# Layer 1 of a two-layer trunk: TensorE takes its work in the order of the program's text

## Chip, core and metric

The kernel runs on one core of a Trainium2 chip. The metric is the device time of one execution in microseconds. Engines are named as in the profile: PE (TensorE, matmuls), DVE (VectorE), ACT (ScalarE), POOL (GpSimd), SP (SyncE, which issues the DMAs).

## What is computed

Two layers over 1024 latent tokens and 256 context tokens, all 1024 wide, in fp32. Layer 0 is attention; layer 1 mixes a bidirectional gated DeltaNet (GDN, 4 heads of 128, chunks of 64 in the reference) with a bidirectional RG-LRU (width 512). Each ends in an output projection, a gate and a LayerNorm. The parts of layer 1 that matter here:

```python
qkv, z, b, a, xr, gr = _split(h @ w_in, REC_SPLITS)       # one input projection
qkv = silu(dwconv_centered(qkv, gdn_conv_w))              # centered, 4 taps
xl  = dwconv_centered(xr, lru_conv_w, lru_conv_b)
# GDN, for both directions:
decay = exp(where(causal, g_cum[..., :, None] - g_cum[..., None, :], -inf))
m   = where(strict, einsum('nbhid,nbhjd->nbhij', kb, k) * decay, 0.0)
sol = triangular_solve(m + eye, [v * beta, kb * exp(g_cum)])
# scan over chunks: v_new = u - w s;  o = q s + attn v_new;  s = s * gl + k_dec^T v_new
# RG-LRU, for both directions: h_t = a_t h_(t-1) + b_t, gates from xl @ w_gate
mix = concatenate([rms_norm(o) * silu(z), r * silu(gr)])
y   = mix @ w_out
```

## The kernel before

Each engine has its own stream of instructions. The program's text emits all of them in one sequence, and the framework's scheduler then makes an order for each engine: it goes by the place in the text but passes over an instruction whose inputs are not ready in the scheduler's own model of time, taking a later one first. `tc.manual_schedule(engines={...})`, entered as a context, switches this off for the engines named: their instructions keep the order of the text. Layer 0's attention already does so for PE and DVE, and closes that context before its output; layer 1 is left wholly to the scheduler.

The text of layer 1 has an order of its own. `seq` lists 24 pieces of the input projection (`xr`, `k`, `q`, `v`, `z`, `gr`, four each). `chunk` (line 1315) computes one piece for one stretch of tokens: 8 times `mm3`, which is three matmuls (high and low parts of the fp32 operands, `h1h`, `h1l`, `wf`), and after each `mm3` a call of `pump()`. That call lets background generators emit a little: first `lru_stream` for either direction (`lx` is the conv output read back from DRAM, `gw` the gate weights, `lw`/`lu` its tiles), then `gdn_prep` (line 1680), then `gdn`'s own levels. A planner with a rough clock for each engine (`Core.t`) decides when a generator may go on.

`gdn_prep` goes over 10 tiles of 128 tokens. For a tile and each direction, one matmul of the mask (`maskr`, `negi`) and one of the tile's decay rows (`dec`, read from the DRAM tensor `d_dec`) make the exponents, and ACT takes `D` = Exp of them. Gram matmuls of keys and queries (`kqt`) follow, and DVE multiplies both into `WX`. SP stores `WX` in `d_w` and, for latent tiles, `d_xa`. `dec` and `kqt` have two buffers each, so a tile's load waits until the tile before last has been read. After five tiles (0 to 4, 5 to 9) eight loads `ia` take the 32x32 diagonal blocks from `d_w`, and `inverse` (line 1780) inverts them, one direction on DVE and the other on POOL, step by step with `ia` and `itmp`; `it` is the transposed copy, stored as `d_bt`. The scan then loads `W`, `Tt`, `Tu`, `K`, `X`, `V`, combines blocks into 64x64 and larger inverses (`Tt,W`, `K,L`, `X,L`), and runs along the tokens with the state `S`. The output projection reads `wo`, `mh` and `ml`.

Other names: `xb` is a projection copied out of PSUM by ACT for the convolution, `yc` the convolution, `tm` a tile for results of z, gr and v (DVE evicts PSUM into it), `wf` the split weights (ACT rounds, DVE or POOL subtracts), `wfs` the weights as loaded. All compute instructions carry line 88, the helper that records them.

Of the kernel before, what the change touches and what calls it, by code (L numbers as in the profile page):

```python
# [111 lines left out]
class Trunk:  # L112
# [1164 lines left out]
    def layer1(self, es, eh):  # L1277
# [48 lines left out]
        def project(i, n0, evac):  # L1326
            for c in range(n0, 3):
                chunk(i, c, evac)
                if c == n0:
                    split(i + 2)  # L1330
                    load(i + 3)
                self.tick()
                self.pump()
# [11 lines left out]
        def copy_to(xb):  # L1345
            def evac(c, t0, n, acc):
                o = (1, 260, 772)[c]
                nc.scalar.copy(xb[:, o:o + n], acc[:, :n])

            return evac  # L1350

        def lru_input(f, xb):
            y = self.til(cp, [P, 1288], F32, "yc", bufs=3)
            self.conv(y, xb, 0, 1283, [rT[:, 48 + 4 * j + f:49 + 4 * j + f] for j in range(4)], rT[:, 64 + f:65 + f])
            nc.sync.dma_start(d["xl"][f, :, 0:256], y[:, 0:256])
            nc.sync.dma_start(d["xl"][f, :, 256:], y[:, 259:1283])
            self.xl_done.add(f)
# [26 lines left out]
        ef.close()  # L1384
        G = self.gdn(es)
        self.add(self.background(G))
        for i, (nm, f) in enumerate(seq):
            if i < 2:
                continue
            if nm in ("z", "gr"):  # L1390
                def evac(c, t0, n, acc):
                    if nm == "gr":
                        hs = self.til(cp, [P, 1288], F32, "yc", bufs=3)[:, 0:1024].rearrange("p (r t) -> p r t", r=2)
                        nc.sync.dma_start(hs, d["hs"][:, f, :, t0 - NCTX:t0 - NCTX + n].rearrange("r p t -> p r t"))
                        nc.vector.tensor_tensor(hs[:, 0], hs[:, 0], hs[:, 1], op=ALU.add)
                    zo = self.til(cp, [P, 512], F32, "tm", bufs=2)
                    nc.scalar.activation(zo[:, :n], acc[:, :n], AF.Tanh, scale=0.5)
                    nc.vector.scalar_tensor_tensor(zo[:, :n], zo[:, :n], 1.0, acc[:, :n], op0=ALU.add, op1=ALU.mult)
                    if nm == "gr":
                        nc.vector.tensor_tensor(zo, zo, hs[:, 0], op=ALU.mult)  # L1400
                    nc.sync.dma_start(d["z" if nm == "z" else "ylru"][f, :, t0 - NCTX:t0 - NCTX + n], zo)

                while nm == "gr" and not {(f, 0), (f, 1)} <= self.lru_done:
                    self.nc.t["p"] += 500.0
                    self.pump()
                project(i, 1, evac)
                continue
            n0 = 1 if nm == "q" else 0
            xb = xbs[:, i % 3]
            project(i, n0, copy_to(xb))  # L1410
            if nm == "xr":
                lru_input(f, xb)
            else:
                self.gdn_inputs(cp, nm, f, n0, xb)
            if f == 3 and nm == "k":
                self.defer(5, lambda: self.gdn_decay(cp))
            if f == 3 and nm == "q":
                self.q_done = True
                self.defer(5, lambda: self.gdn_scale(cp))
# [822 lines left out]
```

## Time and profile before

| | |
|---|---|
| time, median of 3 runs | 1845.74 us (1842.92 to 1847.27) |
| the profiled execution's own time | 1839.24 us |
| its span | 1837.5 us |
| mean granted clock of PE | 0.946 |
| busy: PE | 1657.8 us (90%) |
| busy: DVE | 1206.1 us (66%) |
| busy: ACT | 739.6 us (40%) |
| busy: POOL | 794.9 us (43%) |

The profile is one execution with every instruction's start and duration on its engine, and for idle time the event that ended it. The chain that ended last, followed back from the last instruction, lies 55% on PE and 20% on DVE. The change concerns what is emitted from about 1144 us on. In a timeline row, "[6.07 <-DMA dec<-d_dec]" means 6.07 us of idle time of that engine before the instruction, ended by that DMA; `x2` folds two instructions of one kind. In the page the granted clock is a share of full speed: 1.00 is 2.4 GHz, 0.50 is 1.2 GHz.

### The profile page before, as it was taken

What the parts mean: (1) busy time and instruction counts of PE and PEld (TensorE: products, weight loads), DVE (VectorE), ACT (ScalarE), POOL (GpSimd) and SP (SyncE); (2) the same over time, 40 slices, a digit from 0 to 9 for tenths busy, and PEclk for the clock granted to TensorE, in tenths of its full rate; (3) what the DMA queues carried; (4) which work ended last, traced back from release to release, by engine and by line L of the source; (5) the groups of instructions that cost most, each with busy time, mean ns of one, the idle gap of its engine ahead of it and who ended that gap; (6) DMA issues with size and microseconds to landing.
All of it is one profiled execution on the core that took longest, in us unless ns stands there. A gap on an engine that the chain in (4) does not pass through costs nothing.

```text
span 1837.5 us, 25439 instructions
## 1 busy us (share of the span) xinstructions
PE 1657.8 (90%) x9020; PEld 1210.1 (66%) x9020; DVE 1206.1 (66%) x2140; ACT 739.6 (40%) x1502; POOL 794.9 (43%) x727
## 2 busy tenths in 40 slices
PE   5999899997999998989989998988979858899997
PEld 2997776744555565655547886766856747789885
DVE  2657713236667767676774895888855498367887
ACT  2533401144555453434352443767643222234431
POOL 1432200075566666767542572233212673674121
PEclk8999999998999898989899998989988979999999
DMA  8343486163231101010044333333437447988552
GB/s 303 113 131 115 134 289 198 68 168 114 76 69 56 40 21 45 21 45 27 18 143 143 111 107 99 114 107 123 132 109 198 133 102 211 290 252 252 172 155 103
DMA packets 240995, 234.72 MB, mean 128 GB/s; under 512 B 62506, under 2 KB 188984, under 8 KB 238820
## 3 DMA queue, kind: packets, MB, share of 16 engines
q1 hardware_dynamic: 240868, 233.10, 41.6%
q8 instruction: 71, 1.16, 0.3%
q14 instruction: 56, 0.46, 0.1%
HBM read 163.37 MB, written 69.68 MB: 127 GB/s over the span
## 4 chain that ended last, share of the span: by engine, by line
PE 55%; DVE 20%; DMA 7%; issue 6%; ACT 4%; POOL 4%; SPq 2%; DVEq 0%; ACTq 0%; POOLq 0%
PE ps L88 39%; PE pb L88 10%; PE pv L88 7%; DVE yc L88 3%; DVE nb L88 2%; DVE f L88 2%; DMA modw<-in_mod_w 2%; DVE itmp L88 1%; DVE ia L88 1%; POOL ia L88 1%; DVE mx L88 1%; POOL itmp L88 1%; DVE lu L88 1%; DVE nsq L88 1%; DVE accv L88 1%
## 5 line engine op out<-in xcount | busy, mean ns | idle before, releaser
L88 DVE TENSOR_REDUCE mx<-ps 128x1 f32<-128x512 f32 (+1 forms) x384 | 207.3, 593 | 162.1 <-PE ps L88 160.1
L88 POOL TENSOR_TENSOR accp<-accp,pt 128x512 f32<-128x512 f32 x202 | 260.7, 1313 | 103.7 <-ACT pt L88 102.6
L88 ACT ACTIVATE pt<-pb 128x512 f32<-128x512 f32 (+1 forms) x352 | 194.5, 577 | 229.1 <-PE pb L88 225.0
L88 PE MATMUL ps<-h1h,wf 128*128 128x512 f32 (+1 forms) x864 | 277.9, 395 | 5.8 <-DVE tm L88 3.3
L88 PE MATMUL pb<-qh,kb 96*128 96x512 f32 (+4 forms) x528 | 213.2, 418 | 3.0 <-ACT pt L88 2.3
L88 PEld LDWEIGHTS ps<-h1h,wf 128*128 128x128 f32 x864 | 165.0, 197 | 41.7 <-issue 5.4
L88 PE MATMUL ps<-h1l,wf 128*128 128x512 f32 (+1 forms) x432 | 165.4, 383 | 0.0
L88 PEld LDWEIGHTS pb<-qh,kb 128*128 128x128 f32 (+2 forms) x528 | 102.3, 195 | 90.5 <-issue 65.5
L88 PE MATMUL ps<-kb,qh 128*128 128x512 f32 (+3 forms) x416 | 128.6, 386 | 32.0 <-DVE mx L88 28.7
L88 PE MATMUL pb<-ql,kb 66*128 66x512 f32 (+3 forms) x352 | 139.3, 397 | 0.0
L88 PEld LDWEIGHTS ps<-kb,qh 128*128 128x128 f32 (+1 forms) x416 | 80.9, 201 | 69.3 <-DVE mx L88 37.8
L88 POOL TENSOR_TENSOR accp<-pt,pt 128x512 f32<-128x512 f32 (+1 forms) x47 | 53.0, 1146 | 142.0 <-ACT pt L88 125.4
L88 DVE SCALAR_TENSOR_TENSOR yc<-xb,rT,yc 128x1283 f32<-128x1283 f32 (+1 forms) x48 | 88.1, 1845 | 26.8 <-ACT yc L88 26.4
L88 POOL TENSOR_TENSOR ml<-m,mh 128x512 fp32r<-128x512 f32 (+1 forms) x24 | 49.0, 2053 | 115.0 <-ACT mh L88 105.9
L88 PEld LDWEIGHTS ps<-h1l,wf 128*128 128x128 f32 x432 | 85.5, 198 | 16.7 <-issue 3.9
L88 PE MATMUL ps<-wl,hh 128*128 128x416 f32 (+2 forms) x240 | 84.6, 353 | 8.0 <-POOL wl L88 4.1
L88 PE MATMUL ps<-wh,hh 128*128 128x416 f32 (+2 forms) x240 | 85.4, 356 | 3.1 <-ACT wh L88 2.0
L88 PE MATMUL pv<-pt,vm 128*64 128x512 f32 (+1 forms) x352 | 85.1, 601 | 2.6 <-DVE mo L88 1.7
L88 PE MATMUL pv<-pt,vgqa 128*64 128x512 f32 (+1 forms) x352 | 85.3, 607 | 0.0
L88 PE MATMUL ps<-wh,hl 128*128 128x416 f32 (+2 forms) x240 | 84.0, 350 | 0.1
L88 PE MATMUL ps<-wo,mh 128*128 128x512 f32 x256 | 81.9, 398 | 2.0 <-ACT wo L88 1.6
L88 PE MATMUL ps<-w,mh 128*128 128x512 f32 x256 | 81.3, 398 | 1.1 <-DVE r L88 1.1
(373 smaller groups left out, 3723.9 us busy)
## 6 DMA issues: line engine op xcount, KB each, us to landing
modw<-in_mod_w SPq DMA_DIRECT2D x16, 1024.0 KB
wfs<-in_rec_w_in SPq DMA_DIRECT2D x22, 512.0 KB
modw<-in_mod_w SPq DMA_DIRECT2D x16, 512.0 KB
wst<-in_att_w_in SPq DMA_DIRECT2D x24, 256.0 KB
d_q<-qo SPq DMA_DIRECT2D x20, 256.0 KB
lx<-d_xl SPq DMA_DIRECT2D x8, 640.0 KB
d_w<-WX SPq DMA_DIRECT2D x20, 256.0 KB
W<-d_w SPq DMA_DIRECT2D x20, 256.0 KB
```

Of the source, the lines that this page charges most:

```text
L88: return fn(*args, **kw)
```

## The change

One line is added to `layer1`, after the first two pieces of the projection and after the background work has been registered:

```diff
@@ -1384,6 +1384,7 @@
         ef.close()
         G = self.gdn(es)
         self.add(self.background(G))
+        es.enter_context(self.tc.manual_schedule(engines={mybir.EngineType.PE}))
         for i, (nm, f) in enumerate(seq):
             if i < 2:
                 continue
```

`es` is the outermost context of the program, so this holds to its end: the rest of the input projection, the LRU, the GDN and the output. PE's instructions then stand as the text emits them. The other engines remain with the scheduler, whose model of time sees another PE, so that their orders change too, though not by rule. Numbers in the names below are those of the program's buffers; from about 9980 on those of the new program are higher by two. Line numbers after 1387 are higher by one.

PE, first tiles of `gdn_prep`. In the kernel before, a mask matmul of each direction, then projections and Gram products:

```order
L88 MATMUL ps_11492<-h1h_8679,wf_11157 128x512
L88 MATMUL ps_11496<-maskr_9582,negi_9580 128x512
L88 MATMUL ps_11501<-maskr_9582,negi_9580 128x512
L88 MATMUL ps_11492<-h1h_8679,wf_11157 128x512
L88 MATMUL ps_11492<-h1l_8680,wf_11157 128x512
L88 MATMUL ps_11492<-h1h_8679,wf_11157 128x512
L88 MATMUL ps_11511<-kqt_11482 128x128 x2
```

Further down in the same stream, where the decay matmuls of tiles 0 (`dec_11484`) and 1 (`dec_11489`) stand, and the transposes of a convolution (`ident`, `yc`) among them:

```order
L88 MATMUL ps_11492<-h1h_8679,wf_11157 128x512
L88 MATMUL ps_11567<-kqt_11487 128x128 x2
L88 MATMUL ps_11496<-dec_11484 128x512
L88 MATMUL ps_11501<-dec_11484 128x512
L88 MATMUL ps_11580<-ident_66,yc_11282 128x128 x2
L88 MATMUL ps_11542<-dec_11489 128x512
L88 MATMUL ps_11580<-ident_66,yc_11282 128x128 x2
```

In the changed kernel, the same place:

```order
L88 MATMUL ps_11494<-h1h_8679,wf_11159 128x512
L88 MATMUL ps_11498<-maskr_9582,negi_9580 128x512
L88 MATMUL ps_11498<-dec_11486 128x512
L88 MATMUL ps_11503<-maskr_9582,negi_9580 128x512
L88 MATMUL ps_11503<-dec_11486 128x512
L88 MATMUL ps_11494<-h1h_8679,wf_11159 128x512
L88 MATMUL ps_11494<-h1l_8680,wf_11159 128x512
L88 MATMUL ps_11494<-h1h_8679,wf_11159 128x512
L88 MATMUL ps_11513<-kqt_11484 128x128 x2
L88 MATMUL ps_11494<-h1h_8679,wf_11159 128x512
L88 MATMUL ps_11494<-h1l_8680,wf_11159 128x512
```

Tile 0's two `dec` matmuls moved up directly behind their `maskr`, ahead of 33 other matmuls or folds of matmuls.

SP, the stores of tile 3 (`WX_11698`, `WX_11699`) and the first of tile 4 (`WX_11747`); `dec_11848` is the decay load of tile 7 and `dec_11908` that of tile 8. Before:

```order
L1759 DMA d_w_8691<-WX_11698 128x4x128
L1761 DMA d_xa_8692<-WX_11698 512x1x128
L1759 DMA d_w_8691<-WX_11699 128x4x128
L1761 DMA d_xa_8692<-WX_11699 512x1x128
L1722 DMA kqt_11846<-d_kT_8689 128x4x128
L1725 DMA dec_11848<-d_dec_95 16x640 x2
L1727 DMA kqt_11846<-d_qT_8690 128x4x128
L1725 DMA dec_11908<-d_dec_95 16x640
L1759 DMA d_w_8691<-WX_11747 128x4x128
L1761 DMA d_xa_8692<-WX_11747 512x1x128
```

In the changed kernel, where tile 3 is `WX_11700` and `WX_11701` and tile 7 is `dec_11850`:

```order
L1726 DMA dec_11787<-d_dec_95 16x640
L1723 DMA kqt_11785<-d_kT_8689 128x4x128
L1726 DMA dec_11787<-d_dec_95 16x640
L1728 DMA kqt_11785<-d_qT_8690 128x4x128
L1726 DMA dec_11850<-d_dec_95 16x640
L1760 DMA d_w_8691<-WX_11700 128x4x128
L1762 DMA d_xa_8692<-WX_11700 512x1x128
L1760 DMA d_w_8691<-WX_11701 128x4x128
L1762 DMA d_xa_8692<-WX_11701 512x1x128
```

Half of tile 7's decay load moved ahead of tile 3's stores.

DVE, the end of its inverse: `ia_12201` is the second inverse's matrix, `tm_13036` an eviction of the gr projection and `wf_13157` a split of weights. Before:

```order
L88 SCALAR_TENSOR_TENSOR tm_13036<-tm_13036,ps_13008 128x512
L88 TENSOR_TENSOR ia_12201<-ia_12201,itmp_2957_12883 80x27x4
L88 TENSOR_TENSOR tm_13036<-tm_13036,yc_13033 128x512
L88 TENSOR_TENSOR itmp_2962_12908<-ia_12201 80x84
L88 MEMSET ia_12201 80x32
L88 TENSOR_TENSOR ia_12201<-ia_12201,itmp_2962_12908 80x28x3
L88 TENSOR_TENSOR itmp_2963_12917<-ia_12201 80x58
L88 TENSOR_TENSOR ia_12201<-ia_12201,itmp_2963_12917 80x29x2
L88 TENSOR_TENSOR itmp_2964_12926<-ia_12201 80x30
L88 TENSOR_TENSOR wf_13157<-wfs_13044,wf_13157 128x1024
L88 TENSOR_TENSOR ia_12201<-ia_12201,itmp_2964_12926 80x30
L88 COPY it_12937<-ia_12201 80x1024
```

In the changed kernel (`ia_12203`, `tm_13038`, `wf_13159`):

```order
L88 TENSOR_TENSOR itmp_2962_12910<-ia_12203 80x84
L88 MEMSET ia_12203 80x32
L88 TENSOR_TENSOR ia_12203<-ia_12203,itmp_2962_12910 80x28x3
L88 TENSOR_TENSOR itmp_2963_12919<-ia_12203 80x58
L88 TENSOR_TENSOR ia_12203<-ia_12203,itmp_2963_12919 80x29x2
L88 TENSOR_TENSOR itmp_2964_12928<-ia_12203 80x30
L88 TENSOR_TENSOR ia_12203<-ia_12203,itmp_2964_12928 80x30
L88 COPY it_12939<-ia_12203 80x1024
L88 SCALAR_TENSOR_TENSOR tm_13006<-tm_13006,ps_12954 128x512
L88 SCALAR_TENSOR_TENSOR tm_13038<-tm_13038,ps_13010 128x512
L88 TENSOR_TENSOR tm_13038<-tm_13038,yc_13035 128x512
L88 TENSOR_TENSOR wf_13159<-wfs_13046,wf_13159 128x1024
```

Three evictions into `tm` and one `wf` moved from before the last `it` copy to behind it.

Three more places on PE are told in words. At the first LRU stream, the six fp32 gate matmuls (`ps<-lx,gw`), which stood behind 23 projection matmuls, stand behind the first of 512 columns. In one step of the scan, four matmuls `X,L` and `K,L` stand ahead of 16 `Tt,W` that were ahead of the first `K,L`. In the output, `wo,mh` and `wo,ml` of one output come together, and eight matmuls `S,qq` that stood between them come after.

## Rows read from the trace of the kernel before

**Rows 1.** What PE waited for, 1144 to 1837 us: total us, times, longest us.

```profile
PE ps L88 <- DVE tm L88: 23.8, 6, 17.4
...
PE ps L88 <- ACT xb L88: 6.6, 8, 1.6
```

**Rows 2.** Timeline of PE at the gates: start, us; in brackets idle and releaser.

```profile
1144.71 0.63 PE L88 MATMUL ps<-h1l,wf 128*128 128x512 f32 x1
...
1150.48 0.39 PE L88 MATMUL ps<-h1h,wf 128*128 128x512 f32 x1
1150.71 4.46 PE L88 MATMUL ps<-lx,gw 128*128 128x256 f32 x12
```

**Rows 3.** Busy time by windows: each engine's us, PE's clock, DMA share, GB/s.

```profile
1149.00:1150.00 1.00, 1.00 (x6) 0.83 (x5) 0.93 (x7) 0.00 (x0) 0.00 (x0) 1.00 0.10 21
```

**Rows 4.** Timeline of PE around the first dec load.

```profile
1342.75 0.40 PE L88 MATMUL ps<-maskr,negi 128*128 128x512 f32 x1
1344.13 0.49 PE L88 MATMUL ps<-maskr,negi 128*128 128x512 f32 x1 [0.98 <-ACT jk L88]
...
1349.89 0.50 PE L88 MATMUL ps<-maskr,negi 128*128 128x512 f32 x1 [1.61 <-ACT xb L88]
1350.88 0.60 PE L88 MATMUL ps<-maskr,negi 128*128 128x512 f32 x1 [0.48 <-DVE tm L88]
...
1356.16 0.71 PE L88 MATMUL ps<-kqt 128*128 128x128 f32 x4 [0.67 <-ACT xb L88]
1362.94 1.34 PE L88 MATMUL ps<-dec 16*128 16x512 f32 x2 [6.07 <-DMA dec<-d_dec]
```

**Rows 5.** Windows after two of PE's waits, columns as in rows 3.

```profile
1362.90:1372.00 9.10, 8.92 (x26) 6.01 (x27) 5.65 (x12) 4.97 (x14) 0.00 (x0) 0.52 0.36 84
1372.00:1380.00 8.00, 7.40 (x33) 4.96 (x34) 3.33 (x9) 1.84 (x7) 0.00 (x0) 1.00 0.56 152
1507.00:1516.00 9.00, 7.67 (x22) 5.64 (x23) 8.79 (x16) 2.37 (x7) 8.29 (x10) 0.56 0.76 196
```

**Rows 6.** Timeline of ACT, the decay of tile 2.

```profile
1378.80 1.08 ACT L88 ACTIVATE D<-ps 128x512 f32<-128x512 f32 x2
```

**Rows 7.** Timeline of DVE, WX of tile 2.

```profile
1381.31 2.05 DVE L88 SCALAR_TENSOR_TENSOR WX<-ps,g_s,D 128x256 f32<-128x256 f32 x5 [5.84 <-PE ps L88]
```

**Rows 8.** Timeline of SP's queue, the first stores of tiles 3 and 4.

```profile
1391.70 0.38 SPq L1759 DMA_DIRECT2D d_w<-WX  x1
...
1402.13 0.38 SPq L1759 DMA_DIRECT2D d_w<-WX  x1
```

**Rows 9.** The chain that ended last, 1330 to 1837 us: start, us, what.

```profile
1404.54 0.84 SPq L1786
...
1461.77 3.86 DMA d_xa<-WX
...
1472.09 3.24 DMA ia<-d_w
...
1482.27 0.75 DVE ia L88
...
1556.83 5.15 DMA Tt<-d_bt
...
1739.74 84.46 PE ps L88 x392
```

**Rows 10.** Timeline of DVE in its inverse, two of the evictions between.

```profile
1538.67 1.21 DVE L88 TENSOR_TENSOR wf<-wfs,wf 128x1024 fp32r<-128x1024 f32 x1
...
1545.29 0.69 DVE L88 SCALAR_TENSOR_TENSOR tm<-tm,ps 128x512 f32<-128x512 f32 x1
```

**Rows 11.** Timeline of PE, a step of the scan and the output.

```profile
1605.10 0.60 PE L88 MATMUL ps<-Tt,W 32*32 32x32 f32 x32
1609.76 0.49 PE L88 MATMUL ps<-K,L 128*128 128x128 f32 x2 [4.06 <-POOL K L88]
...
1737.92 0.83 PE L88 MATMUL ps<-S,qq 128*128 128x128 f32 x6
```

## Prediction, made before the result was known

> **What bounds the kernel now.** Read first who TensorE (PE) waits for after 1144 us, where the change begins. Two sums stand out: DVE's `tm` rows, 23.8 us in six waits, and ACT's `xb` copies, 6.6 us in eight short ones [rows 1]. Then the chain of waits, backwards. Its last long piece is PE alone, 84.46 us from 1739.74 on [rows 9]: whatever PE gains or loses there reaches the end undiminished. Before it stands the preparation of the delta rule, one string of steps: decay rows to DRAM, `dec` back, PE's decay matmuls, Exp into `D` on ACT, `WX` on DVE, `d_w` stores and `ia` loads on SP (the load at 1404.54 lies on the chain), the inverses, and the `Tt` load at 1556.83 for which PE waits [rows 9]. So two prices must be kept apart: what the new order does to that string, and what it does to PE's other work, which may fall behind by as much as PE later waits. The largest such wait, 17.44 us, ends at 1507 us and is most of the `tm` sum [rows 1].
>
> The trace does not time a move of the order. What follows puts the rows' durations into the new order by hand. The set of instructions stays the same; 208 of PE's 7430 matmuls change place, in ten stretches, and the schedules of the other engines shift a little with them.
>
> **The change part by part.**
>
> *A, the LRU gates at 1145 us.* Now: 23 projection matmuls run while `lx` is on its way, then the gate matmuls take 4.46 us from 1150.71, without a wait [rows 2]. In the new order the gates follow the first 512-column matmul at 1144.71 and so stand before the load has come. By the DMA engines' share, down to 0.10 in the microsecond from 1149 [rows 3], `lx` lands at about 1149.2. PE then idles about 4.2 us (bounds 3.5 and 6.0, the latter from the gates' present start), and the 23 projections run after. The gates themselves come about 1.4 us earlier. Covered: before 1260 PE waits for ACT and DVE anyway, so its lag is spent there; the LRU scans, on a nearly full DVE, may profit. I take 0, bounds −1.4 and +1.5. Without that cover it would be the whole 4.2 us.
>
> *B, tiles 0 to 2 at 1343 to 1380 us.* The first `dec` load is what PE waits for until 1362.94 [rows 4]. It hangs on rows computed from decay values, stored and read back, none of which waits for PE after 1342 us; it comes when it came. In the present order PE does other things meanwhile: from 1342.75 to 1362.94, that is 20.2 us, it idles 0.98 + 1.61 + 0.48 + 0.67 + 6.07 = 9.8 us [rows 4] and works about 10. In the new order the matmul that needs `dec` stands right behind the first `maskr`, and everything queued behind it, some 30 projection and Gram matmuls, waits: one stall of about 20 us. About 10 us of work is pushed behind it. Of these, 4.6 us ran before 1349.9 and 5.9 after, the latter at a clock that had partly fallen, so that at full rate it is about 7.5. I price it at full rate: after the present stall the granted clock is 0.52, close to the 1.2 GHz level, for 9.1 us and then 1.00 [rows 5], and I expect the same slow stretch after the longer stall, with more of it filled.
>
> Three things come back. PE's short waits for `xb` copies (6.6 us in eight [rows 1]) shrink: about 1 us until tile 3, leaving 6.5. In tile 2 nothing is lost: its `WX` starts only at 1381.31, after 5.84 us of idle DVE [rows 7], since ACT does other reads ahead of the two `D` at 1378.80 [rows 6]; the new order of ACT takes `D` first, and 6.5 us of PE lag put tile 2's `WX` at 1378 to 1381. And tile 6's second decay matmul no longer follows nine projections of 0.23 us each (the step from 1150.48 to 1150.71 [rows 2]), 2.1 us.
>
> Then SP's order decides. The `d_w` stores of tile 3 leave at 1391.70 and those of tile 4 at 1402.13 [rows 8]. In the new order tile 3's stand behind a `dec` load of tile 7, whose buffer is released by PE's tile 5; tile 4's stand, as before, behind one of tile 8, released by PE's tile 6. Tile 4's stores therefore come 6.5 − 2.1 = 4.4 us later, and with them the `ia` loads, now at 1404.54 [rows 9]. Bounds: 0, if tile 2's head start lasts, and +6.5, without the 2.1.
>
> *C, the two inverses, 1404 to 1562 us.* The 4.4 us pass through POOL's inverse into SP's queue, hence to `d_xa` (1461.77), to `WX` of tile 9 and to the second `ia` loads, which land at 1475.33 (1472.09 + 3.24 [rows 9]). DVE's inverse starts at 1482.27 [rows 9], 6.9 us after, because convolutions stand ahead of it. Landing at 1479.8 is still in time; the convolutions slip only as far as they stand behind `WX`: 0 to +3.3, taken as +1.5. Inside the inverse the new order of DVE is lighter: four evictions that stood before the last `it` copy, three of 0.69 us and a `wf` of 1.21 [rows 10], stand behind it, 3.2 us, while one `wf` of 1.21 that ran before the inverse now runs in it: −2.0. Then SP does one or two more issues ahead of the `W` and `Tt` loads, +0.7. PE's projections lag by up to 5 us here, since `tm` comes later between the inverse's steps, but they would end near where `Tt` lands. Sum: +1.5 − 2.0 + 0.7 = +0.2, bounds −2 and +2.
>
> *D, the scan and the output, from 1605 us.* At 1605.10, 32 small `Tt,W` matmuls take 0.60 us under a wait for `K` that ends at 1609.76 [rows 11]. Half of them now stand behind that wait; bounds 0.3 and 0.6, taken 0.5, as they restart after idling. At 1737.92 six `S,qq` matmuls (0.83 us [rows 11]) and two more fill PE's waits for the `wo` weights; in the new order all of one output's `wo` matmuls go first and those eight follow. PE waits just as long and does them later: +0.9 (bounds 0.6 and 1.2). Both are on the bare PE tail.
>
> **The sum**: 0 + 0.2 + 0.5 + 0.9 = +1.6 us; B is inside C, through the start of the inverse. On the profiled execution's 1839.2 us that is 1840.8; the median of the runs lies 6.5 us higher, at 1845.7, so I predict 1847.3.
>
> **A rule on the clock.** The rows show the rate staying low for about 9 us after a wait of 6.07 us [rows 4, 5], and also about as long after one of 17.44 (0.56 from 1507 to 1516 [rows 5]): the longer wait did not cost more. The Trainium skill, "TensorE: Matmul & The Clock Gate", section "What's actually happening", says that the throttled rate is the default and that activity releases it. By that rule a stall of 20 us in one piece speaks against this change; the trace agrees on the drop, and not that a longer stall makes a longer slow stretch.
>
> **The rivals.**
>
> *The lag goes through, slower.* Place: DVE's start of the inverse. If its convolutions all stay behind tile 9's `WX`, the whole 4.4 us arrive, and if the tiles' `tm` evictions fill the place of the four moved ones, the 2.0 are lost: 4.4 + 0.7 + 1.4 = +6.5, or 1852.2. It decides from `WX` of tile 9 starting over 4 us later. For: PE is on the chain almost unbroken after the `dec` wait. Against: 6.9 us of room before the inverse.
>
> *The slow clock lasts, slower still.* If the work pushed behind the stall runs at half rate throughout, PE loses 10 and not 7.5 us, and the moved weights slow the neighbours: about 2.5 to 3.5 us more on top of that rival, 1855. Against it stands the wait of 17.44 us. The rule named above is the one that speaks for it.
>
> *The decays first, faster.* If ACT's and SP's new order puts tile 2's `WX` at 1378, 3.3 us early, and the lead holds to tile 4, the inverse starts no later and loses the four evictions (−3.2) with the `wf` outside: −3.3 − 3.2 + 0.7 + 1.4 = −4.4, or 1841.3. For: DVE idles 5.84 us there [rows 7]. Against: PE itself is the late one in tiles 3 and 4.
>
> *It does next to nothing.* 208 matmuls out of 7430, all in stretches with waits at both ends: stalls are only renamed, +0, 1845.7.
>
> **How the numbers follow.** Chances: forecast 0.40, lag through 0.22, slow clock 0.08, decays first 0.22, nothing 0.08. The forecast's own bounds (A −1.4 to +1.5, C −2 to +2, D 0.9 to 1.8) give 1843.2 to 1851.0; a sixth of it lies past +3.7 us. With 0.2% being 3.7 us, about what a measurement of this kernel can tell from no change, faster has 0.23, same 0.43, slower 0.34. The range runs from 1841 (decays first, its centre) to 1855 (slow clock), leaving out about one in ten at either end.
>
> **What would show it.** In the changed kernel's rows: one PE wait for `dec` of 18 to 21 us ending near 1362.5; a wait of about 4 us before the gates near 1149; `D` of tile 2 near 1376; tile 4's `d_w` stores near 1406.5; POOL's `ia` start 4 us later; the last `it` copy of DVE within 2 us of where it was; no `S,qq` between the `wo` matmuls near 1738. A `dec` that lands much earlier, or an inverse that starts over 4 us away from 1482, would make the prediction wrong.

## The result and the profile after

The changed kernel takes 1861.0 us (median of 7 runs, 1852.53 to 1864.78), the kernel before 1847.27 (7 runs, 1842.92 to 1852.6). The ratio is 1.0087, with a 95% interval of 1.0064 to 1.011: slower by about 16 us by the ratio (the two medians lie 13.7 us apart). The prediction was 1847.3 with a range up to 1855, so the time lies outside it. The profiled execution took 1862.47 us at a mean granted clock of 0.936; the one of before took 1839.24 at 0.946, which is below each of its 7 timed runs. The traces therefore stand 23.2 us apart, some 7 more than the timed runs; the section on the hardware says where a part of that comes from.

The page of the changed kernel, its span and PE's busy time (us, share, instructions):

```profile
span 1860.7 us, 25450 instructions
...
PE 1659.2 (89%) x9020; PEld 1210.0 (65%) x9020; DVE 1211.1 (65%) x2140; ACT 740.2 (40%) x1502; POOL 793.5 (43%) x727
```

PE is busy 1.4 us longer than before and the span is 23 longer. So PE does hardly more work on the whole; it waits more. Its waits from 1144 us to the end (us in total, times, the longest):

```profile
PE ps L88 <- DVE wf L88: 20.4, 1, 20.4
PE ps L88 <- DMA dec<-d_dec: 17.6, 1, 17.6
...
PE ps L88 <- ACT lw L88: 11.0, 1, 11.0
PE ps L88 <- DMA lx<-d_xl: 5.9, 1, 5.9
PE ps L88 <- DVE tm L88: 5.6, 3, 2.8
...
PE ps L88 <- POOL L L88: 4.0, 1, 4.0
```

Against [rows 1], the wait for `dec` in one piece and the one for `lx` are there as foretold. The eight `xb` waits, 6.6 us, have shrunk to two of 2.1 us in all. Where the old kernel waited 17.44 us for `tm`, during the inverse, there are now 20.4 us for `wf`. New and not foretold is the wait for `L`.

To see where the shift arises, the same instruction was looked up in both traces at nine places, and the growth of its lateness noted from one to the next. The places: a DVE step at 1143 us (`halfb`), the gate matmuls of the second LRU stream (1229.48 before), a late convolution (1346.99), the first `WX` of tile 4 (1395.14), DVE's inverse (`ia`, 1482.27), its last `it` copy (1549.22), the start of the scan (the first copy of `S`, 1597.46), the first and last `wo` matmul (1722.50, 1824.48). "Own" means that the order at this place is the text's; a dash means that it is the scheduler's. The prediction gave +4.4 at tile 4 and +1.5 at the inverse, hence the −2.9 between them.

| stretch (before, us) | predicted | after | x1 | x2 | x3 | x4 | y1 | y2 | y3 | z2 | w2 | w3 |
|---|---|---|---|---|---|---|---|---|---|---|---|---|
| own order at: gates (A) | | own | own | – | – | – | – | – | moved | – | moved | – |
| own order at: tiles and inverses (B, C) | | own | – | own | own | – | 0–7 | 8, 9 | own | 0–9 | own | – |
| own order at: scan, output (D) | | own | – | own | – | own | – | – | own | – | own | output |
| 1143 to 1229 | 0 | 7.3 | 8.5 | −0.8 | −0.5 | −0.4 | −0.6 | −0.9 | 0.3 | −0.2 | 1.3 | 0 |
| 1229 to 1347 | 0 | 0 | 0 | 0 | 0 | 0 | −0.1 | 0 | −3.0 | −0.1 | −3.0 | 0 |
| 1347 to 1395 | 4.4 | 3.8 | 5.6 | 2.6 | 3.6 | 5.6 | 2.6 | 6.1 | 3.6 | 2.5 | 3.2 | 0.7 |
| 1395 to 1482 | −2.9 | −2.3 | −0.8 | −2.2 | −2.5 | −0.6 | 0.8 | −3.9 | −2.4 | −2.3 | −2.6 | 0 |
| 1482 to 1549 | −2.0 | −0.8 | 0.2 | −0.9 | −1.0 | 0.6 | 0.1 | 0 | −0.7 | 1.5 | 1.4 | 1.0 |
| 1549 to 1597 | 0.7 | 9.1 | 0.2 | 7.7 | 8.2 | 0.8 | 0.9 | 8.6 | 8.3 | 1.7 | 0.2 | 0.5 |
| 1597 to 1722 | 0.5 | 0.6 | −0.5 | 0.5 | 1.3 | 3.0 | 0.7 | 0.6 | 0.2 | −0.3 | 1.4 | 1.9 |
| 1722 to 1824 | 0.9 | 5.3 | 0.8 | 2.8 | 1.5 | 2.0 | −0.5 | 0.8 | 2.9 | 1.7 | 2.1 | 3.1 |

In the column of the changed kernel two stretches hold 16.4 of 23 us: the one behind the gates, and the one from the last `it` copy to the scan. Both were priced near nothing. The kernels x1 to w3 are those of the next section; the columns of three more (z1, z3, w1) are left out and told of there.

**Behind the gates.** PE's timeline of the changed kernel (start, us, engine, operation, count, idle time before and what ended it), three sets of gate matmuls with the projection ahead of the first:

```profile
1144.88 0.39 PE L88 MATMUL ps<-h1h,wf 128*128 128x512 f32 x1
1151.19 6.09 PE L88 MATMUL ps<-lx,gw 128*128 128x256 f32 x12 [5.92 <-DMA lx<-d_xl]
...
1165.99 4.46 PE L88 MATMUL ps<-lx,gw 128*128 128x256 f32 x12
...
1237.05 1.22 PE L88 MATMUL ps<-lx,gw 128*128 128x256 f32 x2 [11.04 <-ACT lw L88]
```

The same three stood at 1150.71 [rows 2], 1159.81 and 1229.48. The first gates run at the lower rate, 6.09 us against 4.46. The second ones have no wait ahead of them: PE comes to them 6.2 us late, because the 23 projections that used to fill the wait now stand between. Who waits for them is seen in ACT's waits from 1144 to 1229 us, after and before:

```profile
ACT lw L88 <- PE ps L88: 7.2, 9, 3.6
```

```profile
ACT lw L88 <- PE ps L88: 0.6, 2, 0.4
```

The longest of the waits that the prediction counted as cover is PE's for `lw`. In the kernel before:

```profile
1229.48 1.22 PE L88 MATMUL ps<-lx,gw 128*128 128x256 f32 x2 [8.04 <-ACT lw L88]
```

It has not shrunk by the lag: it is 11.04 us and ends 7.6 us later. It is the end of the same string, gates, ACT, DVE's scan and convolutions, ACT, that the lag has delayed. A wait can only absorb a delay if what ends it does not depend on the delayed work.

Not all of the 7.3 us is lag. DVE's `lx` step that stood at 1204.99 is 4.7 us late, counted from the start of the stretch. The other 2.6 us arise behind it, from a new order on DVE: a scan now stands ahead of two convolutions `yc` for which ACT's `xb`, and behind it the gates, wait. DVE after, then before:

```profile
1228.52 2.35 DVE L88 TENSOR_TENSOR_SCAN lw<-lv,lw,lu 128x1024 f32<-128x1024 f32 x1
1230.78 3.12 DVE L88 SCALAR_TENSOR_TENSOR yc<-xb,rT,yc 128x1283 f32<-128x1283 f32 x2
```

```profile
1224.81 1.52 DVE L88 SCALAR_TENSOR_TENSOR yc<-xb,rT,yc 128x1283 f32<-128x1283 f32 x1
1226.25 2.33 DVE L88 TENSOR_TENSOR_SCAN lw<-lv,lw,lu 128x1024 f32<-128x1024 f32 x1
```

The three kernels with the gates moved up (the changed one, x1 and w1) all have this order and lose 2.6 us by it; none of the others has it.

**From the inverse to the scan.** ACT, DVE and PE of the changed kernel, one fence each:

```profile
1574.28 0.60 ACT L88 ACTIVATE tm<-ps 128x512 f32<-128x512 f32 x1 [10.00 <-DMA d_ylru<-tm]
1574.90 1.10 ACT L88 COPY zz<-ps 32x128 f32<-32x128 f32 x4
```

```profile
1579.66 0.69 DVE L88 SCALAR_TENSOR_TENSOR tm<-tm,ps 128x512 f32<-128x512 f32 x1 [3.34 <-ACT tm L88]
1583.75 0.69 DVE L88 TENSOR_TENSOR yc<-yc 128x512 f32<-128x512 f32 x1 [3.41 <-DMA yc<-d_hs]
1584.47 0.28 DVE L88 TENSOR_SCALAR L<-ps 32x128 f32<-32x128 f32 x1
```

```profile
1570.00 0.72 PE L88 MATMUL ps<-Tt,W 32*32 32x32 f32 x32
...
1575.20 0.49 PE L88 MATMUL ps<-zz,Tu 32*32 32x32 f32 x3 [1.54 <-ACT zz L88]
...
1584.90 1.08 PE L88 MATMUL ps<-L,W 64*64 64x64 f32 x8 [3.96 <-POOL L L88]
```

And the two steps of before that answer to the last rows, on DVE and on PE:

```profile
1567.79 0.61 DVE L88 TENSOR_SCALAR L<-ps 32x128 f32<-32x128 f32 x2 [6.97 <-PE ps L88]
```

```profile
1570.74 0.96 PE L88 MATMUL ps<-L,W 64*64 64x64 f32 x16
```

Before, `L` followed PE's `zz,Tu` at once: DVE had waited 6.97 us for them. Now evictions of the `gr` pieces stand ahead: ACT's `tm` waits 10.00 us for a store to free its buffer and holds `zz` back, and DVE's `tm` and `yc`, which wait for ACT and for a load, hold `L` back. ACT's `zz` copies what PE's `Tt,W` made from 1570.00 on and starts 0.02 us after that `tm` ends; `L` starts 0.03 us after that `yc` ends, over 9 us after PE's `zz,Tu` began. So a step of the critical string that is ready waits behind an eviction that is not. `L` goes from 1567.79 to 1584.47, 16.7 us, of which about 8 were there at the last `it` copy (7.3 + 3.8 − 2.3 − 0.8).

The chain that ended last (start, us, what):

```profile
1413.65 0.84 SPq L1787
...
1491.30 0.68 DVE ia L88
...
1741.34 6.12 DMA m<-in_rec_w_out
...
1758.85 88.54 PE ps L88 x400
```

They answer to 1404.54, 1482.27 and 1739.74 in [rows 9]. The last piece, bare PE, starts 19.1 us late and is 4.1 us longer.

### The profile page after: what moved, and what is told of

Its sections match the earlier page's. It is cut to its first block, busy times and chain, and to the rows that moved or that the text cites. A ratio compares the mean times of both kernels' runs of the same rounds, so it can differ in the third digit from the quotient of the medians.

```text
span 1860.7 us, 25450 instructions
## 1 busy us (share of the span) xinstructions
PE 1659.2 (89%) x9020; PEld 1210.0 (65%) x9020; DVE 1211.1 (65%) x2140; ACT 740.2 (40%) x1502; POOL 793.5 (43%) x727
## 5 line engine op out<-in xcount | busy, mean ns | idle before, releaser
L88 PE MATMUL ps<-h1h,wf 128*128 128x512 f32 (+1 forms) x864 | 280.4, 396 | 23.6 <-DVE wf L88 20.4
L88 POOL TENSOR_TENSOR wf<-wfs,wf 128x1024 fp32r<-128x1024 f32 x14 | 42.1, 3010 | 103.3 <-ACT wf L88 93.4
```

What stands on the lines that cost most here:

```text
L88: return fn(*args, **kw)
```

## The experiments

Every ratio is to the kernel before, timed in turn with it; 0.1% is 1.8 us.

**The parts.** x1 has the text's order only until the first `k` piece, where the gates are the one thing that moves on PE. x2 has it from there to the end, x3 from there to the end of the projection, x4 only behind it (entered ahead of `for _ in G`). The edit of x1; the others enter or close the same context at another line:

```diff
         self.add(self.background(G))
+        order = ExitStack()
+        order.enter_context(self.tc.manual_schedule(engines={mybir.EngineType.PE}))
         for i, (nm, f) in enumerate(seq):
...
                 continue
+            if i == 4:
+                order.close()
             if nm in ("z", "gr"):
```

x1: 

> PE keeps the order of the text only through the last two xr pieces, so only the six gate matmuls of the first LRU stream move. Theory 1 (the shift of 7.6 us that the changed kernel shows from 1229 us on was lost at the gates and is never given back): 6 to 8 us slower than the kernel before, 0.3 to 0.45%, PE waits 5 to 6 us for lx. Rival (the prediction's view: later waits swallow the lag): within 1.5 us of the kernel before.

x2: 

> The order of the text begins only with the k pieces, so the gates stay where they were and all other moves of the change are made. Theory 1: 14 to 16 us minus the 7 of the gates, that is 6 to 9 us slower than before (0.3 to 0.5%). Rival (the loss is in gdn_prep and the tail, the gates cost nothing): as slow as the whole change, 14 to 16 us.

x3: 

> The order of the text from the k pieces to the end of the preparation (dec, kqt, the inverses) and not in the scan and the output. Theory 1: 4 to 8 us slower (PE's projections lag behind the second inverse and the gr evictions hold up the first L). Rival (the prediction's working: lag absorbed by 6.9 us of room before the inverse): 0 to 1 us slower.

x4: 

> The order of the text only in the scan and the output: 16 Tt,W behind K,L and 16 S,qq behind the wo matmuls. Theory 1 (the profiles differ there by 5.3 us, of which a slower first weight load is part): 2 to 4 us slower. Rival (the prediction's two terms): 1.4 us slower. Either is near what can be told from no change; the rows at the wo matmuls decide.

| | ratio to before | 95% interval |
|---|---|---|
| x1 | 1.0030 | 1.0007 to 1.0053 |
| x2 | 1.0033 | 1.0008 to 1.0057 |
| x3 | 1.0035 | 1.0013 to 1.0058 |
| x4 | 1.0020 | 0.9998 to 1.0041 |

By the medians, x1 to x4 cost 5.5, 6.1, 6.5 and 3.7 us, all four at or inside what theory 1 said. The intervals exclude the rivals of x2 and x3; that of x1 starts at 1.3 us, just inside its rival's range, and that of x4 excludes neither theory. The parts x1, x3 and x4 sum to 0.85%, the whole is 0.87%. But x2, which has what x3 and x4 have, took 0.33% and not 0.55%, so that the losses add exactly is not shown. One set of gate matmuls, moved ahead of 23 projections, costs from 0.30% (x1) to 0.54% (the whole less x2), as much as all of the middle part or more. In the trace x1 loses 8.5 us in the first stretch, where the prediction had nothing, and gives nothing back.

**Within the middle, and the gates put back.** y1 has the text's order for tiles 0 to 7 (the first two `v` pieces), y2 for tiles 8 and 9 (the next two). y3 is the whole change, with the planner told to emit the first gates later, so that they stand behind the projections again:

```diff
-                yield from self.wait(2500.0)
+                yield from self.wait(2500.0 if dr or f else 6500.0)
```

y1: 

> The order of the text only while the first two v pieces are emitted: decay and Gram matmuls of tiles 0 to 7 move as in the change, the long wait for dec included; tiles 8 and 9, DVE's order in its inverse, the gates and the tail stay as before. Theory 2 (the stall at dec pays for itself, because the work behind it is dense and the clock comes back sooner; the loss of the stretch from k to the preparation's end comes later): between 5 us faster and 1 us slower than before, PE waiting 17 to 18 us for dec. Rival (the prediction's lag goes through: stores of tile 4 late by 4.4 us): 4 to 6 us slower, with the ia loads late by as much.

y2: 

> The order of the text only while the last two v pieces are emitted: 39 matmuls of tiles 8 and 9 move on PE, and with them the orders of DVE and ACT from the second inverse on become those of the change; dec wait, gates and tail as before. Theory 2 (the gr evictions that stand ahead of the first L on DVE, and PE's projections behind a late wf, are the loss of that stretch): 5 to 8 us slower, the first L,W of PE later by that much after the last it copy. Rival (39 matmuls at two tiles carry nothing): within 1 us of before.

y3: 

> The whole change, but the text lets the first LRU stream wait longer for lx, so that its six gate matmuls are emitted at the place where the scheduler had put them; the planner then places other LRU steps a little differently. Theory 1 (the stall for lx costs 5 to 9 us): 5 to 9 us faster than the whole change, that is 7 to 11 us slower than before, no wait of PE for lx. Rival (the loss belongs to the order of the text as such and moves elsewhere): as the whole change, 14 to 16 us slower than before.

y1 took 1.0022 (0.9999 to 1.0046), y2 1.0013 (0.9991 to 1.0036), y3 1.0040 (1.0020 to 1.0060). PE's gates in y3:

```profile
1149.35 4.53 PE L88 MATMUL ps<-lx,gw 128*128 128x256 f32 x12 [0.53 <-DMA lx<-d_xl]
```

The wait is 0.53 us and the first stretch costs 0.3. The second gives 3.0 back, in y3 and in w2, which has the same edit: later LRU steps stand in another order there, and that gain is no part of the change undone. The interval of y3 ends at 1.0060, that of the whole change starts at 1.0064: the gates' place is shown to be a large part of the loss, 0.47% with that gain in it; y3's 7.4 us lie in theory 1's range. The split of the middle is shown by the table: y1 alone loses little from 1549 to 1597 (0.9), and y2 alone the whole 8.6. The loss before `L` comes from the order in the pieces of tiles 8 and 9, with the orders that DVE and ACT then get, and not from the stall for `dec`. The times of y1 and y2 can't be told apart from no change. By its median y1 costs 4.1 us, which misses theory 2 and lies in the rival's range, though the rival's sign is not there: tile 4's stores leave 0.3 us late, not 4.4. The median of y2, 2.4 us (interval to 6.6), lies between its two theories, below the 8.6 of its trace, which had gained 3.9 us ahead of the inverse.

**The slow clock, and the evictions.** z1 is y1 with 70 further mask matmuls ahead of the first `dec`, overwritten by the one that counts, so that PE works through the wait. z2 has the text's order for tiles 0 to 9 and one more edit: the weights of the second `z` piece (the expectations say the third) are split, and the next ones loaded, ahead of the first chunk of the last `v` piece and not behind it. The scheduler then puts `L` on DVE ahead of the evictions that held it back. z3 has both. The edit of z1, then that of z2:

```diff
                 pd = self.ps([P, 4, P])
...
+                for _ in range(70 if t == 0 and dr == 0 else 0):
+                    self.mm(pd, self.negi, self.mr[:, dr].unsqueeze(1).broadcast_to([P, 4, P]), True, True)
...
                 self.mm(pd, self.negi, self.mr[:, dr].unsqueeze(1).broadcast_to([P, 4, P]), True, False)
```

```diff
             for c in range(n0, 3):
+                if c == n0 and 15 <= i < 16:
+                    split(i + 2)
+                    load(i + 3)
                 chunk(i, c, evac)
-                if c == n0:
+                if c == n0 and not 15 <= i < 16:
                     split(i + 2)
```

z1: 

> As the kernel with the order of the text for tiles 0 to 7 only, and PE is kept busy in its wait of 17.6 us for dec by 70 extra mask matmuls of 512 columns whose results are overwritten. If the half rate after the wait (8 us of it) is what the stall costs, PE's granted clock is 1.00 behind the wait and WX of tile 4 comes 2 to 4 us earlier than without the extra matmuls: within 1 us of the kernel before, or up to 3 us faster. If the order, and not the clock, costs the 4 us measured there: as without them, 3 to 5 us slower than before. If the matmuls overrun the wait, dec's matmuls start late by that.

z2: 

> The order of the text for all four v pieces (tiles 0 to 9), gates and tail as before, and one weight split (that of the third z piece) and its next load stand one chunk earlier in the text. On DVE this split then stands before the inverse, and the first L evictions stand ahead of the later gr evictions again. Theory 2 (the 8 us between the last it copy and the scan come from PE's long wait for that split and from evictions ahead of L): those 8 us shrink to under 3, and the kernel is 0 to 4 us faster than before. Rival (the loss is PE's backlog from the tiles, whatever DVE's order): 5 to 7 us slower, as the order of the text from k to the preparation's end was.

z3: 

> The earlier split and the 70 extra mask matmuls together. If both theories hold: 2 to 6 us faster than before (0.1 to 0.3%), the lead visible at WX of tile 4 and kept to the scan. If either is wrong, no faster than the better of the two alone.

z1 took 1.0022 (0.9999 to 1.0045), z2 1.0014 (0.9991 to 1.0038), z3 1.0013 (0.9990 to 1.0037). PE in z1, and the first `WX` of tiles 3 and 4 on DVE:

```profile
1349.41 16.28 PE L88 MATMUL ps<-maskr,negi 128*128 128x512 f32 x71
1367.44 0.50 PE L88 MATMUL ps<-dec 16*128 16x512 f32 x1 [1.75 <-DMA dec<-d_dec]
```

```profile
1395.83 0.88 DVE L88 SCALAR_TENSOR_TENSOR WX<-ps,g_s,D 128x256 f32<-128x256 f32 x2 [3.74 <-DMA d_xa<-WX]
...
1404.52 0.88 DVE L88 SCALAR_TENSOR_TENSOR WX<-ps,g_s,D 128x256 f32<-128x256 f32 x2 [4.53 <-DMA d_xa<-WX]
```

The wait is filled and `dec` runs at full rate (0.50 us instead of 0.79), yet `WX` of tile 4 is late by 2.7 us, as in y1 (2.6): `WX` waits for the stores of its own buffers. The slow clock is not gone: the granted clock is 0.50 for 3.4 us from 1369.5, against 5.6 us in y1. What z1 saves of it makes tile 3's `WX` 1.1 us earlier than y1's and does not reach tile 4; so much of the slow clock does not set the tiles. By its median z1 costs 4.1 us, the range named for the order and not the clock. In z2, `L` on DVE:

```profile
1572.17 0.61 DVE L88 TENSOR_SCALAR L<-ps 32x128 f32<-32x128 f32 x2 [8.58 <-PE ps L88]
```

DVE waits for PE again, as before, and the stretch costs 1.7 instead of 8 to 9 us. The edit also removes PE's long wait for `wf` (20.1 us in y2, 20.3 in x3; in z2 the longest wait there is 13.0, for `tm`), behind which the later projections, and so their evictions, stand. So the late split and the evictions that it brings ahead of `L` are the cause there, together; z2 does not part them. The timed intervals of z2 and x3 overlap; for this place alone the trace speaks, not the time. z2 was expected 0 to 4 us faster than before and z3 2 to 6; their medians are 2.6 and 2.4 us slower, and that gain did not come.

**Two repairs, and the rest.** w1 is x1 with 24 mask matmuls in the wait for `lx`, which asks whether the gates' slow rate or PE's backlog (the projections that come after the wait) costs. w2 is the whole change with the repairs of y3 and z2. w3 has the text's order only from the start of the output projection. The edits of w1 and w3:

```diff
                     acc = self.ps([P, 512])
...
+                    for _ in range(24 if (dr, f, c, g) == (0, 0, 0, 0) else 0):
+                        self.mm(acc, self.negi, self.mr[:, 0].unsqueeze(1).broadcast_to([P, 4, P]), True, True)
```

```diff
             if i == 8:
+                es.enter_context(self.tc.manual_schedule(engines={mybir.EngineType.PE}))
                 tail = output()
```

w1: 

> As the kernel in which only the gates move (0.30% slower than before), and PE is kept busy in its wait for lx by 24 extra mask matmuls of 512 columns whose results are overwritten, so that the gates run at full rate (4.5 us in place of 6.1). If the clock is the larger part of the gates' loss: within 2 us of before. If PE's backlog (its projections come after the wait, and the xb copies and convolutions wait for them) is the larger part: 4 to 6 us slower than before, with the second stream's gates at 1229 us still 5 us or more late against the first ones.

w2: 

> The whole change with its two dear places mended in the text: the first gates are emitted where the scheduler had put them, and the split of the third z piece one chunk earlier, so that the first L stands ahead of the gr evictions. If these two places carry the loss: 2 to 5 us slower than before (what the output's order and the tiles cost is left), against 14 to 16 for the change. If the loss has other sources: 7 us or more slower, as with the gates alone mended.

w3: 

> The order of the text only from the ninth step of the scan on: the 16 S,qq behind the wo matmuls, and not the 16 Tt,W in the scan. If the tail's 0.20% is the output's: 2 to 4 us slower than before, the first wo matmul to the last one 2 us or more longer. If it is the scan's: within 1 us of before.

w1 took 1.0044 (1.0023 to 1.0065). PE in w1, whose profiled execution runs some microseconds late before the change begins:

```profile
1154.83 5.65 PE L88 MATMUL ps<-maskr,negi 128*128 128x512 f32 x24
1160.73 4.53 PE L88 MATMUL ps<-lx,gw 128*128 128x256 f32 x12 [0.26 <-DMA lx<-d_xl]
```

The gates run at full rate, 4.53 us instead of x1's 7.53, and the first stretch still loses 5.6 us. So by these two traces 2.9 of x1's 8.5 us go to the rate. Of the 5.6 that are left, 2.6 are DVE's new order, which w1 has too, and 3.0 the stall and PE's backlog: three parts of like size, and none of them the larger part that the expectation asked for. The time does not show the saving: w1's median is 8.1 us slower than before, above both of its ranges and above x1's 5.5, with overlapping intervals.

w2 took 1.0018 (0.9992 to 1.0043), w3 1.0011 (0.9985 to 1.0036). Two small moves take the change from 0.87% back to where it can't be told from no change, 3.3 us by the median as expected: the two places are the bulk of the loss, even if the 3.0 us (0.16%) that y3's edit gains elsewhere are added back. w3's 2.0 us (−2.8 to 6.6) does not tell the output from the scan. No version was measured faster than the kernel before.

## Why the prediction was wrong

**A, the gates.** The stall was foretold at 4.2 us (bounds 3.5 and 6.0) and measured 5.92. The load was put at 1149.2 by the DMA engines' share. It became usable at 1151.19, while the share of the changed kernel fell thus (the last three columns of a window: granted clock, DMA share, GB/s):

```profile
1149.00:1150.00 1.00, 0.00 (x0) 0.00 (x0) 0.94 (x7) 0.00 (x0) 0.00 (x0) 0.50 0.34 96
1150.00:1151.00 1.00, 0.00 (x0) 0.00 (x0) 1.00 (x3) 0.00 (x0) 0.00 (x0) 0.50 0.07 20
```

That error is small. The step of the prediction that failed is "Covered: before 1260 PE waits for ACT and DVE anyway, so its lag is spent there", with its bounds of −1.4 and +1.5. The shift measured 7.3 us: 4.7 of lag that went along the LRU's own string, and 2.6 from DVE's new order, in which an LRU scan, which the prediction had down as a possible gain, holds up the convolutions. The next sentence had the alternative, "Without that cover it would be the whole 4.2 us", but no rival and no part of the range was made from it. It was also missed that the gates themselves would run at half rate behind the stall, and that a second set of gates stands behind the 23 projections.

**B, the tiles.** Here the wait was as foretold, and only a part of the path behind it:

```profile
1368.35 0.79 PE L88 MATMUL ps<-dec 16*128 16x512 f32 x1 [17.59 <-DMA dec<-d_dec]
```

Less the 7.6 us that the trace is late by then, it ends at 1360.8, near the 1362.5 foretold. Tile 4's stores were to be 4.4 us late. Its `WX` is, by 3.8; the stores and then the `ia` loads (1413.65 against 1404.54) are late by 9.1 − 7.6 = 1.5 only. DVE's inverse (1491.30 against 1482.27) is late by 1.4 beyond A; 1.5 was foretold. That this agrees is luck: the 1.5 was to be what is left of 4.4 us on tile 9's `WX`, and that `WX` is late by 0.4 only, while the convolutions ahead of the inverse stand in another order.

**C, the inverses.** Inside the inverse −0.8 against −2.0: a small miss. The second step that failed is "PE's projections lag by up to 5 us here ... but they would end near where `Tt` lands", with SP's +0.7 as the whole price behind it. It asked about PE alone. The new order had moved evictions behind the last `it` copy, which was booked as a gain, and what they would then stand ahead of was not asked: `zz` and `L`. That is +9.1 us where +0.7 was foretold.

**D, scan and output.** The scan costs 0.6 against 0.5. At the output not eight but 16 `S,qq` come behind the `wo` matmuls, in the changed kernel all of them at a granted clock of 0.50 (1758.5 to 1765.3), behind a wait for weights, in w3 the first of them only (to 1749.5); the changed kernel, then w3:

```profile
1757.00 0.50 PE L88 MATMUL ps<-wo,mh 128*128 128x512 f32 x1 [1.81 <-ACT wo L88]
...
1760.60 3.62 PE L88 MATMUL ps<-S,qq 128*128 128x128 f32 x16
```

```profile
1748.50 2.43 PE L88 MATMUL ps<-S,qq 128*128 128x128 f32 x16
```

The stretch measured 5.3, but this trace also has a long first `wo` load (6.12 us on the chain, against 3.17 for the like piece before). In the five other kernels with the text's order there it measures 2.0 to 3.1 (mean 2.6), and in the eight without it −0.5 to 3.1 (mean 1.3, z1, z3 and w1 among them at 1.5, 3.1 and 1.5). The edit's own price is then about 1.3 us; 0.9 was foretold, and the runs can't tell the two apart.

**The rivals.** "The lag goes through" and "The slow clock lasts" ended on the right side for reasons that did not occur in the changed kernel: the inverse started 1.4 us late beyond A, not 4.4, and the slow stretch ended 8 us after the wait. (In y1, with the order of tiles 0 to 7 alone, 3.4 us did arrive at the inverse.) "The decays first" had its lead, tile 2's `WX` 1.9 us early, but at tile 3 it was 3.5 us late. None of the rivals had the gates or the evictions.

## What to carry to other kernels

A wait of the bounding engine absorbs a delay only if the step that ends it does not itself hang on the delayed work; follow that step back before it is booked as cover. When a reorder moves work out of one critical string, look at what the same queue does next: an eviction that waits for a buffer holds back the ready step behind it (here `zz` and `L`). Look at the other engines' streams too: the order was changed on PE alone, and part of the loss came from what DVE then did first. To keep the text's order here, one would have to emit the gates where their load has come, and the weights of the next piece early enough; w2, which does both, is still not measured faster than the kernel before.

## What the hardware showed

**The slow stretch after one and the same order has two lengths.** The granted clock after the `dec` wait, in the changed kernel (wait of 17.59 us, ended at 1368.35) and in x1, which has the order of before there (wait of 7.18 us, ended at 1366.29):

```profile
1371.40:1374.40 3.00, 3.00 (x11) 2.52 (x11) 1.13 (x4) 0.00 (x0) 0.00 (x0) 0.50 0.10 27
1374.40:1377.40 3.00, 3.00 (x12) 2.26 (x11) 1.13 (x4) 0.00 (x0) 0.00 (x0) 0.70 0.29 75
1377.40:1380.40 3.00, 3.00 (x13) 2.06 (x14) 0.30 (x1) 1.20 (x2) 0.00 (x0) 1.00 1.03 301
```

```profile
1366.30:1369.30 3.00, 2.57 (x6) 1.30 (x7) 1.42 (x6) 1.08 (x2) 0.00 (x0) 0.50 0.31 78
...
1387.30:1390.30 3.00, 3.00 (x8) 2.34 (x7) 2.60 (x7) 1.85 (x8) 0.00 (x0) 0.50 0.34 102
1390.30:1393.30 3.00, 3.00 (x12) 2.02 (x10) 0.63 (x2) 1.09 (x2) 0.00 (x0) 0.89 0.25 75
```

After the longer wait PE is back at 2.4 GHz within some 8 us; in x1 it stays at 1.2 GHz until 1390, some 24 us, with PE busy almost without a gap. With the order of before at this place, the low rate lasted about 9 us in two profiles (before and w3, whose waits were 6.07 and 6.06 us) and some 24 us in four (x1, x4, y2, w1, whose waits were 7.18 to 7.89), and those four lose 5.6 to 6.1 us up to `WX` of tile 4, w3 0.7. In the seven profiles with the text's order and no filling (the changed kernel, x2, x3, y1, y3, z2, w2), with waits of 17.6 to 19.1 us, it was always 5 to 8 us, so the length of the wait alone does not set it. The Trainium skill, "TensorE: Matmul & The Clock Gate", section "What's actually happening", has activity release the low rate; the rows agree on the drop behind a wait, but why the rate came back after 9 us in one run and not in another, they do not show, and it stays open. It may explain a part of the profiled gap: the profile of before is one of the two short ones. In the output, too, it has a granted clock of 1.00 throughout (1722 to 1824), where x1, with the same order, has 0.50 from 1746.0 to 1749.3. Both fit a trace of before that lies under its median, and the prediction added the difference, 6.5 us, as if the changed kernel had it too. Against the four long ones the tiles of the changed kernel lose nothing (3.8 us against 5.6 to 6.1); which of the two lengths the timed runs of before have, the record does not show.

**The run's time goes with the mean clock.** Over 35 runs of the kernel before in one series (1832.54 to 1855.13 us) the correlation of time and mean granted clock is −0.7; in the three other series, of 29 runs each, it is −0.7 to −0.8. Which of the two follows the other, this does not show. A single trace of this kernel can thus lie 6 us from its median, more than most terms of the prediction.
